# Up projection with x stationary, and u turned to channels on partitions by a transposing DMA

## The chip, the cores and the metric

The kernel runs on one core of one Trainium2 chip. The metric is the device time of one execution in microseconds (us), taken as the median of several runs. A profile is one execution recorded by the hardware profiler; its span goes from the first to the last instruction.

## The reference

One encoder layer on 256 tokens of width 2048, in fp32. The part that the change touches is the convolutional gated feed-forward at its end:

```
def conv_gated_ffn(h, w_up, conv_w, conv_b, w_down):     # h = rms_norm(x): (1, 256, 2048)
    u = h @ w_up                                         # w_up: (2048, 11264)
    up_ = jnp.pad(u, ((0, 0), (1, 1), (0, 0)))
    u = up_[:, :-2] * conv_w[0] + up_[:, 1:-1] * conv_w[1] + up_[:, 2:] * conv_w[2] + conv_b
    gate, val = jnp.split(u, 2, axis=-1)
    return (jax.nn.silu(gate) * val) @ w_down            # w_down: (5632, 2048)
```

Ahead of it stand RMS norm, an input projection, window attention over 8 heads, a bidirectional gated linear attention and the output projection `wo`.

## The kernel before

TensorE works with pairs of numbers. Every fp32 operand is split into a rounded part `hi` (type fp32r) and a rest `lo`; a product of two fp32 matrices is three matmuls, hi by hi, hi by lo and lo by hi, summed in PSUM. Weights come from HBM in units of 128 partitions x 1024 columns (512 KB). For each unit `weights()` issues the load on SyncE's queue (tile `r`, four buffers), ScalarE writes `h` (four buffers) and VectorE writes `l` (three buffers). These two instructions are put forward in the schedule by `high_priority`; otherwise the order of each engine's instructions is set at build time by a scheduler from the order of the program, and each engine runs its list in that order.

The stages follow one another on TensorE: ten chunks of the input projection with attention and linear attention between them, `wo`, the up projection, the down projection. In the input projection, `wo` and the down projection a 128x128 block of the activations is stationary and 512 weight columns move. In the up projection it is the other way: 128x128 weight blocks are stationary, so that u comes out with channels on partitions and tokens along the row, as the convolution over tokens wants it. The loop goes over the 44 channel blocks `f` and the two halves (gate and value), 88 blocks of 128 channels, each with 16 blocks of the contraction. For each of these there are two matmuls: the weight's hi part against x's hi and lo side by side (512 columns, L630), and the weight's lo part against x's hi (256 columns, L631). Both write one PSUM tile `pu` of a pool of four.

A block is then finished by one ScalarE copy (L633) and VectorE instructions: the two halves of `pu` are added, the token's norm factor `rbc` is multiplied on (it was spread over the partitions by a small matmul, `pb`), three instructions make the convolution, and then follow SiLU, the product of gate and value, and the split into `g`, which the down projection keeps stationary.

The names in the rows: `hu`, `lu`, `ru` are the parts and the raw tile of a unit of w_up, `hd`, `ld`, `rd` those of w_down; `xs` holds the split x; `ptx` are TensorE transposes of the last columns of `wo`'s result; `u`, `c` are the block before and after the convolution.

Of the kernel before, what the change touches and what calls it, by code (L numbers as in the profile page):

```python
# [8 lines left out]
F32 = mybir.dt.float32  # L9
F32R = mybir.dt.float32r  # L10
BF16 = mybir.dt.bfloat16
U32 = mybir.dt.uint32
AF = mybir.ActivationFunctionType
ALU = mybir.AluOpType
AX = mybir.AxisListType
# [3 lines left out]
P = 128  # L19
T = 256  # L20
DM = 2048
NKT = DM // P
# [4 lines left out]
NFF = DFF // P  # L27
# [32 lines left out]
def tile_hymba_layer(  # L60
# [15 lines left out]
    nc = tc.nc  # L76
    V, S, G, PE = nc.vector, nc.scalar, nc.gpsimd, nc.tensor
# [9 lines left out]
    def arena(shape, dt, name):  # L87
        return ar.tile(shape, dt, name=name, tag="ar")

    def work(shape, dt, name, tag="wk", bufs=2):  # L90
        return wk.tile(shape, dt, name=name, tag=tag, bufs=bufs)

    def acc(name):
        return pacc.tile([P, 512], F32, name=name, tag="acc")

    def aux(name):
        return paux.tile([P, 512], F32, name=name, tag="aux")
# [14 lines left out]
    def split(hi, lo, src):  # L112
        S.activation(hi, src, AF.Copy)
        V.tensor_tensor(lo, src, hi.bitcast(F32), ALU.subtract)
# [56 lines left out]
    def token_square(c):  # L171

        r = raw(f"xq{c}")
        nc.sync.dma_start(out=r, in_=xr[c])
        for t in range(2):
            junk = work([P, 512], BF16, "junkx", "jk", 1)
            S.activation(junk, r[:, t * 512 : t * 512 + 512], AF.Square, accum_out=ssq1[:, t, c : c + 1])

    def token_norm():
# [290 lines left out]
    def retrieve(h):  # L470
        po = aux(f"pog{h}")
        for t in range(2):
            for s in range(2):
                product(
                    po[:, t * T : t * T + T], both(atr, A, h, 2 * s + t), both(vgr, A, s, slice(h * T, h * T + T)),
                    start=(s == 0), stop=(s == 1),
                )
        o = o_sb[:, h]
        S.activation(o.rearrange("p t e -> p (t e)"), po, AF.Copy)
        ss = sm.tile([P, 2], F32, name="sso", tag="sso", bufs=4)  # L480
        rs = sm.tile([P, 2], F32, name="rso", tag="rso", bufs=4)
        for t in range(2):
            junk = work([P, T], BF16, "junko", "jk", 1)
            S.activation(junk, o[:, t], AF.Square, accum_out=ss[:, t : t + 1])
        inv_sqrt(rs, ss, 1.0 / T, EPS, 2)
        yield
        for t in range(2):
            V.scalar_tensor_tensor(
                out=o[:, t], in0=o[:, t], scalar=rs[:, t : t + 1], in1=sg[:, t, h * T : h * T + T], op0=ALU.mult, op1=ALU.mult
            )  # L490
        yield
        pt = aux(f"pto{h}")
        for t in range(2):
            for e in range(2):
                PE.transpose(pt[:, e * T + t * P : e * T + t * P + P], o[:, t, e * P : e * P + P], ident)
        split(ogh[:, 2 * h : 2 * h + 2], ogl[:, 2 * h : 2 * h + 2], pt.rearrange("p (k s) -> p k s", k=2))
# [68 lines left out]
    first = 0  # L565
    for c in range(4):
        xres = raw(f"xres{c}")
        nc.sync.dma_start(out=xres[:, :1024], in_=xr[c])
        ps = [acc(f"po{c}{t}") for t in range(2)]
        for u in range(NKT // 2):  # L570
            if c == 0:
                run_hooks(10, u)
            hi, lo = weights(wo, first, 1024, f"o{c}{u}")
            first += P * 1024
            for k in range(2):
                kt = 2 * u + k
                sh, sl = (oah, oal) if kt < 8 else (ogh, ogl)
                for t in range(2):
                    a = sh[:, kt % 8, t * P : t * P + P]
                    b = sl[:, kt % 8, t * P : t * P + P]  # L580
                    wh, wl = hi[:, k * 512 : k * 512 + 512], lo[:, k * 512 : k * 512 + 512]
                    PE.matmul(ps[t], a, wh, start=(kt == 0), stop=False)  # L582
                    PE.matmul(ps[t], a, wl, start=False, stop=False)  # L583
                    PE.matmul(ps[t], b, wh, start=False, stop=(kt == NKT - 1))  # L584
        x1c = x1[c // 2][:, c % 2]
        for t in range(2):
            V.tensor_tensor(x1c[:, t], ps[t], xres[:, t * 512 : t * 512 + 512], ALU.add)
            junk = work([P, 512], BF16, "junk2", "jk", 1)
            S.activation(junk, x1c[:, t], AF.Square, accum_out=ssq2[:, t, c : c + 1])
        for i in range(2):  # L590
            pt = aux(f"ptx{c}{i}")
            for j in range(2):
                for t in range(2):
                    n = (2 * i + j) * P
                    PE.transpose(pt[:, j * T + t * P : j * T + t * P + P], x1c[:, t, n : n + P], ident)
            for j in range(2):
                n = 4 * c + 2 * i + j
                h = xs[n // 4][:, n % 4, 0]
                S.activation(h, pt[:, j * T : j * T + T], AF.Copy, scale=g2[:, n : n + 1])
                V.scalar_tensor_tensor(  # L600
                    out=xs[n // 4][:, n % 4, 1], in0=pt[:, j * T : j * T + T], scalar=g2[:, n : n + 1],
                    in1=h.bitcast(F32), op0=ALU.mult, op1=ALU.subtract,
                )
# [1 line left out]
    rstd2 = pers.tile([P, 2], F32, name="rstd2")  # L605
    V.tensor_reduce(s2, ssq2, AX.X, ALU.add)
    inv_sqrt(rstd2, s2, 1.0 / DM, EPS, 2)
    pb = aux("pb")
    for t in range(2):
        dg = work([P, P], F32, f"dg{t}")  # L610
        V.tensor_scalar(dg, ident, rstd2[:, t : t + 1], None, op0=ALU.mult)
        PE.matmul(pb[:, t * P : t * P + P], ones, dg, start=True, stop=True)
    rbc = pers.tile([P, T], F32, name="rbc")
    V.tensor_copy(rbc, pb[:, :T])


    gts = [arena([P, 2, 4, T], F32R, f"g{i}") for i in range(NFF // 4)]
    first = 0
    for f in range(NFF):
        cs = []  # L620
        for half in range(2):
            n = f + half * NFF
            pu = acc(f"pu{n}")
            for u in range(2):
                hi, lo = weights(wu, first, 1024, f"u{n}{u}")
                first += P * 1024
                for k in range(8):
                    wh, wl = hi[:, k * P : k * P + P], lo[:, k * P : k * P + P]
                    x2 = xs[2 * u + k // 4][:, k % 4].rearrange("p a s -> p (a s)")
                    PE.matmul(pu, wh, x2, start=(u == 0 and k == 0), stop=False)  # L630
                    PE.matmul(pu[:, T:], wl, x2[:, :T], start=False, stop=(u == 1 and k == 7))  # L631
            ut = work([P, T], F32, f"u{n}", "pT")
            S.activation(ut, pu[:, T:], AF.Copy)  # L633
            V.tensor_tensor(ut, ut, pu[:, :T], ALU.add)  # L634
            V.tensor_tensor(ut, ut, rbc, ALU.mult)  # L635
            c = work([P, T], F32, f"c{n}", "sc", 3)
            V.tensor_scalar(c, ut, cw[:, 1, n : n + 1], cb[:, n : n + 1], op0=ALU.mult, op1=ALU.add)  # L637
            V.scalar_tensor_tensor(  # L638
                out=c[:, 1:T], in0=ut[:, 0 : T - 1], scalar=cw[:, 0, n : n + 1], in1=c[:, 1:T], op0=ALU.mult, op1=ALU.add
            )  # L640
            V.scalar_tensor_tensor(  # L641
                out=c[:, 0 : T - 1], in0=ut[:, 1:T], scalar=cw[:, 2, n : n + 1], in1=c[:, 0 : T - 1], op0=ALU.mult, op1=ALU.add
            )
            cs.append(c)
        S.activation(cs[0], cs[0], AF.Silu)
        V.tensor_tensor(cs[1], cs[0], cs[1], ALU.mult)
        gt = gts[f // 4]
        S.activation(gt[:, 0, f % 4], cs[1], AF.Copy)
        V.tensor_tensor(gt[:, 1, f % 4], cs[1], gt[:, 0, f % 4].bitcast(F32), ALU.subtract)


    first = 0
    for c in range(4):
        ps = [acc(f"pd{c}{t}") for t in range(2)]
        for u in range(NFF // 2):
            hi, lo = weights(wd, first, 1024, f"d{c}{u}")
            first += P * 1024
            for k in range(2):
                kt = 2 * u + k
                gt = gts[kt // 4]  # L660
                for t in range(2):
                    a = gt[:, 0, kt % 4, t * P : t * P + P]
                    b = gt[:, 1, kt % 4, t * P : t * P + P]
                    wh, wl = hi[:, k * 512 : k * 512 + 512], lo[:, k * 512 : k * 512 + 512]
                    PE.matmul(ps[t], a, wh, start=(kt == 0), stop=False)  # L665
                    PE.matmul(ps[t], a, wl, start=False, stop=False)  # L666
                    PE.matmul(ps[t], b, wh, start=False, stop=(kt == NFF - 1))  # L667
# [111 lines left out]
```

## Time and profile before

| | |
|---|---|
| median of 3 runs | 1086.81 us (1085.79 to 1088.91) |
| profiled execution, its own time | 1088.95 us |
| its span | 1087.2 us, 14981 instructions |
| TensorE busy | 1077.7 us (99%) |
| VectorE busy | 769.5 us (71%) |
| ScalarE busy | 535.0 us (49%) |
| DMA | 205.06 MB, 189 GB/s in the mean |
| granted TensorE clock | 0.998 |

Busy time of TensorE counts a matmul until its result has drained, so that neighbours overlap; what a stage costs is read from the starts of its matmuls.

### The profile page before, as it was taken

How to read it: one execution, taken by the hardware profiler on the slowest of the kernel's cores; microseconds unless marked ns; L12 is line 12 of the kernel's file. 1: busy time of each engine (PE TensorE's matmuls, PEld its weight loads, DVE VectorE, ACT ScalarE, POOL GpSimd, SP SyncE). 2: the span in 40 equal slices, each digit the busy share in tenths (PEclk: the TensorE clock that was granted, in tenths of full speed). 3: DMA queues.
4: the chain of work that ended last, by engine and by line, in shares of the span. 5: the costliest groups of instructions: out<-in, count | busy, mean ns of one | idle time of the engine just before them, and what ended most of it. 6: DMA issues, size and time to landing. Idle time of an engine off the chain costs nothing.

```text
span 1087.2 us, 14981 instructions
## 1 busy us (share of the span) xinstructions
PE 1077.7 (99%) x5608; PEld 918.2 (84%) x5608; DVE 769.5 (71%) x1174; ACT 535.0 (49%) x796; POOL 11.3 (1%) x16
## 2 busy tenths in 40 slices
PE   9999999999999999999999999999999999999998
PEld 7789888888888888888888888888888888888886
DVE  6688776755555888888888888888888544444443
ACT  6646575764445544444444444444444433333331
POOL 0010000010000000000000000000000000000000
PEclk9999999999999999999999999999999999999999
DMA  9765545445656656665565565655666666666662
GB/s 343 266 195 163 172 125 161 131 137 191 195 194 224 189 187 189 183 191 182 186 192 182 188 187 183 192 179 189 186 184 192 193 194 211 194 214 194 211 194 80
DMA packets 58616, 205.06 MB, mean 189 GB/s; under 512 B 6640, under 2 KB 7664, under 8 KB 58416
## 3 DMA queue, kind: packets, MB, share of 16 engines
q1 hardware_dynamic: 58256, 203.97, 59.3%
q8 instruction: 44, 0.72, 0.3%
q14 instruction: 28, 0.23, 0.1%
q10 hardware_dynamic: 288, 0.14, 0.0%
HBM read 201.99 MB, written 2.10 MB: 188 GB/s over the span
## 4 chain that ended last, share of the span: by engine, by line
PE 96%; DMA 2%; DVE 1%; ACT 0%; issue 0%; DVEq 0%; SPq 0%; ACTq 0%
PE pu L630 30%; PE pu L631 15%; PE pd L667 7%; PE pd L665 7%; PE pd L666 7%; PE po L583 3%; PE po L584 3%; PE po L582 3%; PE pvg L226 1%; PE pvg L227 1%; PE pgt L228 1%; PE pgt L226 1%; PE pvg L228 1%; PE pgt L227 1%; PE pqa L227 1%; PE pqa L228 1%
## 5 line engine op out<-in xcount | busy, mean ns | idle before, releaser
L630 PE MATMUL pu<-xs,hu 128*128 128x512 f32 x1408 | 497.4, 399 | 0.0
L631 PE MATMUL pu<-xs,lu 128*128 128x256 f32 x1408 | 395.2, 281 | 0.0
L630 PEld LDWEIGHTS pu<-xs,hu 128*128 128x128 f32 x1408 | 264.4, 188 | 65.6
L108 ACT ACTIVATE hu<-ru 128x1024 fp32r<-128x1024 f32 x176 | 186.9, 1062 | 253.4 <-PE pu L630 143.6
L631 PEld LDWEIGHTS pu<-xs,lu 128*128 128x128 f32 x1408 | 266.0, 189 | 0.2
L109 DVE TENSOR_TENSOR lu<-ru,hu 128x1024 fp32r<-128x1024 f32 x176 | 215.2, 1223 | 47.5 <-PE pu L631 41.1
L109 DVE TENSOR_TENSOR ld<-rd,hd 128x1024 fp32r<-128x1024 f32 x88 | 107.8, 1225 | 117.5 <-PE pd L666 114.0
L108 ACT ACTIVATE hd<-rd 128x1024 fp32r<-128x1024 f32 x88 | 93.6, 1064 | 143.8 <-PE pd L667 135.0
L666 PE MATMUL pd<-ld,g 128*128 128x512 f32 x352 | 136.9, 389 | 0.0
L665 PE MATMUL pd<-hd,g 128*128 128x512 f32 x352 | 136.9, 389 | 0.0
L667 PE MATMUL pd<-hd,g 128*128 128x512 f32 x352 | 136.9, 389 | 0.0
L667 PEld LDWEIGHTS pd<-hd,g 128*128 128x128 f32 x352 | 66.1, 188 | 13.8
L666 PEld LDWEIGHTS pd<-ld,g 128*128 128x128 f32 x352 | 66.1, 188 | 13.8
L665 PEld LDWEIGHTS pd<-hd,g 128*128 128x128 f32 x352 | 66.1, 188 | 13.5
L109 DVE TENSOR_TENSOR lo<-ro,ho 128x1024 fp32r<-128x1024 f32 x32 | 38.8, 1223 | 38.4 <-ACT ho L108 27.8
L108 ACT ACTIVATE ho<-ro 128x1024 fp32r<-128x1024 f32 x32 | 33.8, 1060 | 46.4 <-DMA ro<-in_wo_dram 33.0
L634 DVE TENSOR_TENSOR u<-u,pu 128x256 f32<-128x256 f32 x88 | 36.9, 420 | 13.8 <-ACT u L633 13.3
L641 DVE SCALAR_TENSOR_TENSOR c<-u,prm_sb,c 128x255 f32<-128x255 f32 x88 | 42.5, 484 | 3.0
L638 DVE SCALAR_TENSOR_TENSOR c<-u,prm_sb,c 128x255 f32<-128x255 f32 x88 | 41.9, 477 | 0.1
L637 DVE TENSOR_SCALAR c<-u,prm_sb 128x256 f32<-128x256 f32 x88 | 36.2, 412 | 3.0
L635 DVE TENSOR_TENSOR u<-u,rbc 128x256 f32<-128x256 f32 x88 | 37.1, 421 | 1.5
L633 ACT ACTIVATE u<-pu 128x256 f32<-128x256 f32 x88 | 32.1, 365 | 0.0
(221 smaller groups left out, 1390.5 us busy)
## 6 DMA issues: line engine op xcount, KB each, us to landing
ru<-in_wu_dram SPq DMA_DIRECT2D x176, 512.0 KB, 4.0
rd<-in_wd_dram SPq DMA_DIRECT2D x88, 512.0 KB, 4.3
ro<-in_wo_dram SPq DMA_DIRECT2D x32, 512.0 KB, 3.6
riqa<-in_wi_dram SPq DMA_DIRECT2D x16, 512.0 KB, 3.6
rivg<-in_wi_dram SPq DMA_DIRECT2D x16, 512.0 KB, 3.9
rigt<-in_wi_dram SPq DMA_DIRECT2D x16, 512.0 KB, 3.5
riqg<-in_wi_dram SPq DMA_DIRECT2D x8, 512.0 KB, 3.5
rilk<-in_wi_dram SPq DMA_DIRECT2D x10, 408.0 KB, 3.5
```

The lines of the kernel that those rows point to most:

```text
L108: S.activation(hi[:, :cols], r[:, :cols], AF.Copy)
L109: V.tensor_tensor(lo[:, :cols], r[:, :cols], hi[:, :cols].bitcast(F32), ALU.subtract)
L630: PE.matmul(pu, wh, x2, start=(u == 0 and k == 0), stop=False)
L631: PE.matmul(pu[:, T:], wl, x2[:, :T], start=False, stop=(u == 1 and k == 7))
L634: V.tensor_tensor(ut, ut, pu[:, :T], ALU.add)
L635: V.tensor_tensor(ut, ut, rbc, ALU.mult)
L637: V.tensor_scalar(c, ut, cw[:, 1, n : n + 1], cb[:, n : n + 1], op0=ALU.mult, op1=ALU.add)
L638: V.scalar_tensor_tensor(out=c[:, 1:T], in0=ut[:, 0 : T - 1], scalar=cw[:, 0, n : n + 1], in1=c[:, 1:T], op0=ALU.mult, op1=ALU.add)
L641: V.scalar_tensor_tensor(out=c[:, 0 : T - 1], in0=ut[:, 1:T], scalar=cw[:, 2, n : n + 1], in1=c[:, 0 : T - 1], op0=ALU.mult, op1=ALU.add)
L665: PE.matmul(ps[t], a, wh, start=(kt == 0), stop=False)
L666: PE.matmul(ps[t], a, wl, start=False, stop=False)
L667: PE.matmul(ps[t], b, wh, start=False, stop=(kt == NFF - 1))
```

## The change

The up projection is turned round. It goes over 22 chunks `ch` of 512 columns (256 gate channels and the 256 value channels that belong to them; the host orders w_up so). For each chunk a 128-token block of x is stationary and 512 weight columns move, three matmuls for each contraction block and token block, into two PSUM tiles, one for each 128 tokens. The result has tokens on partitions, so the norm factor is a per-partition scale of the evacuation (`us`, ScalarE). To get channels on partitions, VectorE copies the 16-bit halves of each fp32 of `us` into two planes (`pl`, 128 x 1024 of 16 bits), a transposing DMA on ScalarE's queue turns each `pl` (`uT`), and ScalarE writes the two planes back interleaved, which is fp32 again (`v`). The middle tap of the convolution and the bias go to ScalarE, for two blocks of channels there is one SiLU, one product and one split. `turn` of a chunk stands behind unit 1 and `convolve` behind unit 3 of the next chunk; those of the last chunk stand in the first column of the down projection. The matmul `pb` is gone. The pool of scratch tiles has four buffers of tag "wk" in place of two, and the scrap tiles of the squares (`junk`) use it too.

```
-    def work(shape, dt, name, tag="wk", bufs=2):
-        return wk.tile(shape, dt, name=name, tag=tag, bufs=bufs)
+    def work(shape, dt, name, tag="wk", bufs=None):
+        return wk.tile(shape, dt, name=name, tag=tag, bufs=bufs or (4 if tag == "wk" else 2))
...
-            junk = work([P, 512], BF16, "junk2", "jk", 1)
+            junk = work([P, 512], BF16, "junk2")
...
+    def up(ch):
+        ps = [acc(f"pu{ch}{t}") for t in range(2)]
+        for u in range(NKT // 2):
+            hi, lo = weights(wu, ch * DM * 512 + u * P * 1024, 1024, f"u{ch}_{u}")
+            for k in range(2):
+                kt = 2 * u + k
+                wh, wl = hi[:, k * 512 : k * 512 + 512], lo[:, k * 512 : k * 512 + 512]
+                for t in range(2):
+                    a = xs[kt // 4][:, kt % 4, 0, t * P : t * P + P]
+                    b = xs[kt // 4][:, kt % 4, 1, t * P : t * P + P]
+                    PE.matmul(ps[t], a, wh, start=(kt == 0), stop=False)
+                    PE.matmul(ps[t], a, wl, start=False, stop=False)
+                    PE.matmul(ps[t], b, wh, start=False, stop=(kt == NKT - 1))
+            if ch and u == 1:
+                turn(ch - 1)
+            if ch and u == 3:
+                convolve(ch - 1)
...
+            us = work([P, 512], F32, f"us{ch}{t}", "wk", 4)
+            pl = work([P, 2, 512], U16, f"pl{ch}{t}", "wk", 4)
+            with tc.high_priority(offset=1500):
+                S.activation(us, ps[t], AF.Copy, scale=rstd2[:, t : t + 1])
+            V.tensor_copy(pl, us.bitcast(U16).rearrange("p (n h) -> p h n", h=2))
...
+    def turn(ch):
+        ut = work([P, 2, 4, T], U16, f"uT{ch}", "pT")
+        flat = ut.rearrange("p h j s -> p (h j) s")
+        for t in range(2):
+            nc.scalar.dma_start_transpose(flat[:, :, t * P : t * P + P], planes[ch][t].rearrange("p h n -> p (h n)"))
...
+            v = work([P, 2, T], F32, f"v{ch}{half}", "sc", 3)
+            S.activation(
+                v.rearrange("p j s -> p (j s)").bitcast(U16).rearrange("p (n h) -> p h n", h=2),
+                turned[ch][:, :, 2 * half : 2 * half + 2].rearrange("p h j s -> p h (j s)"), AF.Copy,
             )
...
+                S.activation(c[:, j], v[:, j], AF.Identity, bias=cb[:, n : n + 1], scale=cw[:, 1, n : n + 1])
```

On TensorE, in the middle of the up projection, a contraction block of one block of 128 channels took a 512-column and a 256-column matmul:

```order
L630 MATMUL pu_4570<-xs_2461,hu_4573 128x512
L631 MATMUL pu_4570<-xs_2461,lu_4574 128x256
L630 MATMUL pu_4570<-xs_2461,hu_4573 128x512
L631 MATMUL pu_4570<-xs_2461,lu_4574 128x256
L630 MATMUL pu_4570<-xs_2461,hu_4573 128x512
L631 MATMUL pu_4570<-xs_2461,lu_4574 128x256
```

Now a contraction block of four blocks of channels takes six matmuls of 512 columns, three for each token tile; 12 of them belong to one unit of weights:

```order
L626 MATMUL pu_4595<-hu_4_4696,xs_2462 128x512
L627 MATMUL pu_4595<-lu_4_4697,xs_2462 128x512
L628 MATMUL pu_4595<-hu_4_4696,xs_2462 128x512
L626 MATMUL pu_4596<-hu_4_4696,xs_2462 128x512
L627 MATMUL pu_4596<-lu_4_4697,xs_2462 128x512
```

In all there were 2816 matmuls of the up projection, and now there are 2112, all of 512 columns.

On ScalarE, in the middle of the up projection, the list before held two conversions of weights (`hu`) for each block, and between them the copies of `pu` and the work on `c` and `g`:

```order
L633 ACTIVATE u_4725<-pu_4680 128x256
L108 ACTIVATE hu_4850<-ru_4848 128x1024
L108 ACTIVATE hu_4872<-ru_4870 128x1024
L633 ACTIVATE u_4782<-pu_4737 128x256
L648 ACTIVATE g_3189<-c_4729 128x256
```

Now the two evacuations of a chunk, its two transposing DMAs and the joining of its planes stand in one list with the conversions for the next chunk (`hu_3` is unit 3 of that chunk):

```order
L109 ACTIVATE hu_2_3743<-ru_2_3741 128x1024
L638 ACTIVATE us_3692<-pu_3521,rstd_3172 128x512
L109 ACTIVATE hu_3_3761<-ru_3_3759 128x1024
L638 ACTIVATE us_3696<-pu_3522,rstd_3172 128x512
L646 DMA_TRANSPOSE uT_3738<-pl_3693 128x8x128
L109 ACTIVATE hu_4_3801<-ru_4_3799 128x1024
L646 DMA_TRANSPOSE uT_3738<-pl_3697 128x8x128
L109 ACTIVATE hu_5_3819<-ru_5_3817 128x1024
L653 ACTIVATE v_3777<-uT_3738 128x2x512
L660 ACTIVATE c_3779<-v_3777,prm_sb 128x256 x2
L653 ACTIVATE v_3786<-uT_3738 128x2x512
L109 ACTIVATE hu_6_3837<-ru_6_3835 128x1024
```

The conversion of unit 6 moved behind the joining, and the first joining instruction waits for both transposing DMAs.

On VectorE the same stretch of the change has the copies into planes behind `lu_2`, and the convolution between `lu_5` and `lu_6`:

```order
L110 TENSOR_TENSOR lu_2_3744<-ru_2_3741,hu_2_3743 128x1024
L639 COPY pl_3693<-us_3692 128x1024
L639 COPY pl_3697<-us_3696 128x1024
L110 TENSOR_TENSOR lu_3_3762<-ru_3_3759,hu_3_3761 128x1024
L110 TENSOR_TENSOR lu_4_3802<-ru_4_3799,hu_4_3801 128x1024
L110 TENSOR_TENSOR lu_5_3820<-ru_5_3817,hu_5_3819 128x1024
L661 SCALAR_TENSOR_TENSOR c_3779<-v_3777,prm_sb,c_3779 128x255 x2
L664 SCALAR_TENSOR_TENSOR c_3779<-v_3777,prm_sb,c_3779 128x255 x2
L110 TENSOR_TENSOR lu_6_3838<-ru_6_3835,hu_6_3837 128x1024
```

So `lu_6` stands behind instructions that read what the transposing DMAs bring.

## Rows read from the trace of the kernel before

**Rows 1.** The page: busy time of each engine in its span.

```profile
span 1087.2 us, 14981 instructions
PE 1077.7 (99%) x5608; PEld 918.2 (84%) x5608; DVE 769.5 (71%) x1174; ACT 535.0 (49%) x796; POOL 11.3 (1%) x16
```

**Rows 2.** The page: the chain that ended last, by engine.

```profile
PE 96%; DMA 2%; DVE 1%; ACT 0%; issue 0%; DVEq 0%; SPq 0%; ACTq 0%
```

**Rows 3.** TensorE's waits, longest and shortest of six: total us, times, longest us.

```profile
PE pqa L226 <- ACT hiqa L108: 1.5, 1, 1.5
...
PE pkv L227 <- DVE likv L109: 0.5, 1, 0.5
```

**Rows 4.** Windows: stretch, its length, busy us (instructions) of PE, PEld, DVE, ACT, POOL, clock, DMA share, GB/s.

```profile
0.00:40.00 40.00, 35.31 (x146) 27.61 (x147) 21.61 (x35) 27.42 (x50) 0.90 (x5) 0.98 0.88 319
400.00:600.00 200.00, 200.00 (x1133) 173.33 (x1133) 172.22 (x283) 95.49 (x141) 0.00 (x0) 1.00 0.60 187
600.00:622.55 22.55, 22.55 (x129) 19.54 (x129) 19.43 (x33) 10.80 (x16) 0.00 (x0) 1.00 0.59 187
```

**Rows 5.** Timeline of TensorE around the up and down projections: start us, us, instruction.

```profile
345.00 0.39 PE L630 MATMUL pu<-xs,hu 128*128 128x512 f32 x1
...
350.37 0.82 PE L595 MATMUL ptx<-prm_sb,x 128*128 128x128 f32 x6
350.94 0.36 PE L631 MATMUL pu<-xs,lu 128*128 128x256 f32 x1
...
353.46 0.61 PE L612 MATMUL pb<-dg,ones 128*128 128x128 f32 x4
353.83 0.36 PE L631 MATMUL pu<-xs,lu 128*128 128x256 f32 x1
...
843.61 0.40 PE L665 MATMUL pd<-hd,g 128*128 128x512 f32 x1
...
1082.77 0.39 PE L667 MATMUL pd<-hd,g 128*128 128x512 f32 x1
```

**Rows 6.** Timeline of TensorE in the attention: 256-column matmuls one behind another.

```profile
119.82 0.28 PE L120 MATMUL pss<-kvr,qT 128*128 128x256 f32 x1
...
120.18 0.28 PE L120 MATMUL pss<-kvr,qT 128*128 128x256 f32 x1
```

**Rows 7.** Groups, 600 to 622.55 us: busy us, mean ns of one | idle before.

```profile
L108 ACT ACTIVATE hu<-ru 128x1024 fp32r<-128x1024 f32 x8 | 8.5, 1062 | 11.8 <-PE pu L630 7.1 <-issue 4.8
L633 ACT ACTIVATE u<-pu 128x256 f32<-128x256 f32 x4 | 1.5, 364 | 0.0
...
L109 DVE TENSOR_TENSOR lu<-ru,hu 128x1024 fp32r<-128x1024 f32 x8 | 9.8, 1224 | 2.0 <-PE pu L631 2.0
...
L638 DVE SCALAR_TENSOR_TENSOR c<-u,prm_sb,c 128x255 f32<-128x255 f32 x4 | 1.9, 477 | 0.0
```

**Rows 8.** Groups of the whole span with the shapes that the change uses.

```profile
L114 DVE TENSOR_TENSOR pT<-pp,pT 128x512 fp32r<-128x512 f32 x8 | 5.5, 684 | 1.7 <-ACT pT L113 1.7
L113 ACT ACTIVATE pT<-pp 128x512 fp32r<-128x512 f32 x8 | 4.7, 586 | 4.9 <-PE pp L335 4.9
L234 ACT ACTIVATE qa_sb<-pqa,rstd 128x512 f32<-128x512 f32 x4 | 2.7, 686 | 2.6 <-PE pqa L228 2.6
L386 ACT ACTIVATE na<-na 128x512 f32<-128x512 f32 x4 | 2.4, 620 | 2.5 <-DVE na L385 2.5
L390 DVE TENSOR_TENSOR mn<-mn,na 128x1024 f32<-128x1024 f32 x2 | 2.4, 1222 | 1.6 <-ACT na L387 1.6
L392 ACT ACTIVATE gh<-mn 128x1024 fp32r<-128x1024 f32 x2 | 2.1, 1046 | 0.0
```

**Rows 9.** DMA queues (packets, MB, share) and issues (KB each, median us to landing).

```profile
q1 hardware_dynamic: 58256, 203.97, 59.3%
...
ru<-in_wu_dram SPq DMA_DIRECT2D x176, 512.0 KB, 4.0
...
out_dram<-x SPq DMA_DIRECT2D x7, 256.0 KB, 3.6
```

More of the change, by code (lines that the diff above doesn't have):

```diff
@@ L12 @@
 U32 = mybir.dt.uint32
+U16 = mybir.dt.uint16
 AF = mybir.ActivationFunctionType
@@ L175, in token_square @@
         for t in range(2):
-            junk = work([P, 512], BF16, "junkx", "jk", 1)
+            junk = work([P, 512], BF16, "junkx")
             S.activation(junk, r[:, t * 512 : t * 512 + 512], AF.Square, accum_out=ssq1[:, t, c : c + 1])
@@ L482, in retrieve @@
         for t in range(2):
-            junk = work([P, T], BF16, "junko", "jk", 1)
+            junk = work([P, T], BF16, "junko")
             S.activation(junk, o[:, t], AF.Square, accum_out=ss[:, t : t + 1])
@@ L607, in tile_hymba_layer @@
     inv_sqrt(rstd2, s2, 1.0 / DM, EPS, 2)
[L608 to L614, printed above, removed]
-    gts = [arena([P, 2, 4, T], F32R, f"g{i}") for i in range(NFF // 4)]
-    first = 0
-    for f in range(NFF):
+    gts = [arena([P, 2, 4, T], F32R, f"g{i}") for i in range(NFF // 4)]
@@ new lines, in tile_hymba_layer @@
+    planes, turned = {}, {}
+    def up(ch):
[15 more added lines that the diff above has]
+                convolve(ch - 1)
+        planes[ch] = []
+        for t in range(2):
[4 more added lines that the diff above has]
+            V.tensor_copy(pl, us.bitcast(U16).rearrange("p (n h) -> p h n", h=2))
+            planes[ch].append(pl)
@@ L620, in tile_hymba_layer, with convolve @@
+    def turn(ch):
+        ut = work([P, 2, 4, T], U16, f"uT{ch}", "pT")
+        flat = ut.rearrange("p h j s -> p (h j) s")
+        for t in range(2):
+            nc.scalar.dma_start_transpose(flat[:, :, t * P : t * P + P], planes[ch][t].rearrange("p h n -> p (h n)"))
+        turned[ch] = ut
+    def convolve(ch):
         cs = []
         for half in range(2):
[L622 to L639, printed above, removed]
-            )
@@ L641, in tile_hymba_layer @@
-            V.scalar_tensor_tensor(
-                out=c[:, 0 : T - 1], in0=ut[:, 1:T], scalar=cw[:, 2, n : n + 1], in1=c[:, 0 : T - 1], op0=ALU.mult, op1=ALU.add
-            )
+            v = work([P, 2, T], F32, f"v{ch}{half}", "sc", 3)
+            S.activation(
+                v.rearrange("p j s -> p (j s)").bitcast(U16).rearrange("p (n h) -> p h n", h=2),
+                turned[ch][:, :, 2 * half : 2 * half + 2].rearrange("p h j s -> p h (j s)"), AF.Copy,
+            )
+            c = work([P, 2, T], F32, f"c{ch}{half}", "sc", 3)
@@ new lines, in convolve @@
+            for j in range(2):
+                n = half * NFF + 2 * ch + j
+                S.activation(c[:, j], v[:, j], AF.Identity, bias=cb[:, n : n + 1], scale=cw[:, 1, n : n + 1])
+                V.scalar_tensor_tensor(
+                    out=c[:, j, 1:T], in0=v[:, j, 0 : T - 1], scalar=cw[:, 0, n : n + 1], in1=c[:, j, 1:T], op0=ALU.mult, op1=ALU.add
+                )
+                V.scalar_tensor_tensor(
+                    out=c[:, j, 0 : T - 1], in0=v[:, j, 1:T], scalar=cw[:, 2, n : n + 1], in1=c[:, j, 0 : T - 1], op0=ALU.mult, op1=ALU.add
+                )
@@ L646, in tile_hymba_layer @@
         V.tensor_tensor(cs[1], cs[0], cs[1], ALU.mult)
+        f = 2 * ch
         gt = gts[f // 4]
-        S.activation(gt[:, 0, f % 4], cs[1], AF.Copy)
-        V.tensor_tensor(gt[:, 1, f % 4], cs[1], gt[:, 0, f % 4].bitcast(F32), ALU.subtract)
+        split(gt[:, 0, f % 4 : f % 4 + 2], gt[:, 1, f % 4 : f % 4 + 2], cs[1])
+    for ch in range(NFF // 2):
+        up(ch)
     first = 0
@@ L655, in tile_hymba_layer @@
         for u in range(NFF // 2):
+            if c == 0 and u == 1:
+                turn(NFF // 2 - 1)
+            if c == 0 and u == 3:
+                convolve(NFF // 2 - 1)
             hi, lo = weights(wd, first, 1024, f"d{c}{u}")
@@ L742 @@
     w = a["w_up"][0]
-    wu = w.reshape(2, 8, P, 2, NFF, P).transpose(4, 3, 0, 2, 1, 5).reshape(-1)
+    w = w.reshape(DM, 2, NFF // 2, 2 * P).transpose(2, 0, 1, 3).reshape(NFF // 2, DM, 512)
+    wu = np.concatenate([_units(w[c], [2] * (NKT // 2)) for c in range(NFF // 2)])
     w = a["w_down"][0]
```

## The prediction

> **What bounds the kernel now.** The page comes first: TensorE is busy for 1077.7 of 1087.2 us [rows 1], and the chain that ended last runs through TensorE for 96% [rows 2]. Busy time of overlapping matmuls proves little, so the waits come next: TensorE waited for others six times only, 1.5 us at the longest and 0.5 at the shortest, and no instruction of the up projection is among them [rows 3]. The windows show who else is near: in the up projection VectorE is busy for 172 of 200 us, ScalarE for 95, DMA at a share of 0.60 [rows 4]. So this stage goes at the pace at which TensorE issues matmuls at full clock, and a change is worth what it takes from that pace, unless it makes another engine late.
>
> The pace is read from starts. The up projection begins at 345.00, the down projection at 843.61 [rows 5]: 498.61 us. In it lie transposes (six pushed the next matmul back by 0.57 us, so eight by about 0.76) and `pb` (0.37). The other 497.5 us hold 1408 pairs of a 512-column and a 256-column matmul, 353.3 ns a pair. The down projection has 1056 matmuls of 512 columns from 843.61 to 1082.77 [rows 5]: 239.16 / 1055 = 226.7 ns each. Where 256-column matmuls follow each other, three starts take 0.36 us, 120 ns each [rows 6]. At 2.4 GHz the columns alone are 213.3 and 106.7 ns, so each matmul costs 13 ns beyond its columns. A pair would then be 346.7 ns; the up projection pays 6.6 ns more, for which no row names a cause.
>
> **TensorE's part.** The columns stay the same: 1408 x 768 = 2112 x 512. The count falls from 2816 to 2112, 704 fewer, at 13.3 ns 9.4 us. `pb` saves 0.37. What becomes of the unnamed 6.6 ns a pair (9.3 us in all) isn't known. If it goes, the stage takes 2112 x 0.2267 + 0.76 = 479.5 us, 19.1 less. If it stays with the columns, it is 9.3 more: 488.8, 9.8 less. The down projection, whose form the new loop has, doesn't pay it, but VectorE is much quieter there. I take the middle, 484.2 us and a saving of 14.4.
>
> Here a rule of the Trainium skill speaks against the change. The row says that a matmul costs 13 ns over its columns at either width [rows 5, 6]. The page "TensorE: Matmul & The Clock Gate" (Part 1, "Wait — 56ns, not 53.3ns?") gives a fixed cost of about 2.5 ns per warm matmul. By that 704 fewer matmuls would save 1.8 us, by the rows 9.4. The trace doesn't agree with the page for these fp32 operands; the sum goes by the rows.
>
> **VectorE and ScalarE.** A chunk of the change does the work of four blocks, which now last 22.55 us with VectorE busy for 19.43 and ScalarE for 10.80 [rows 4]. New on VectorE: eight `lu` of 1.224, two plane copies priced at the 1222 ns of a 128x1024 instruction, eight convolution taps of 0.477, a product and a split of 0.684 [rows 7, 8]: 9.8 + 2.4 + 3.8 + 1.4 = 17.4 us of a chunk of 22. That is lighter than now. New on ScalarE: eight `hu` of 1.062, two evacuations of 0.686, two joins at 1.046, four middle taps at 0.364, SiLU at 0.620, a split at 0.586 [rows 7, 8]: 8.5 + 1.4 + 2.1 + 1.5 + 0.6 + 0.6 = 14.7 us, and two DMA issues. Neither is full; what these cost is nothing as long as the lists keep their order in time. The traffic grows by 2 x 256 KB a chunk, 24 GB/s on about 190; the first 40 us moved 319 GB/s [rows 4].
>
> **The wait that the change adds.** The join waits for two transposing DMAs, and behind it in ScalarE's list stand `hu_6`, `hu_7`; behind the taps in VectorE's list stands `lu_6`. TensorE waits for those. With 12 matmuls a unit (2.75 us), let a chunk end at 0. `us` of the first token block runs to 0.8, `hu_3`, whose buffer comes free at 0, to 1.9, the second `us` to 2.6; VectorE does `lu_2` to 1.3, plane copies to 2.5 and 3.8. So the first DMA is issued at 2.6 and, with `hu_4` between them, the second at 3.8. On the other side: TensorE begins unit 6 at 16.5, so `hu_6` has to be done by about 15.5 for `lu_6` to follow. Ahead of it are join, two taps, join (2.8 us) and itself (1.06): the DMAs must have landed by 11.6 us.
>
> No row shows a transposing DMA. From below: 256 KB at the 319 GB/s of the first stretch are 0.8 us. From above: 58256 packets took 59.3% of 16 engines' 1087.2 us [rows 1, 9], 0.177 us each. Cut into 256-byte pieces (128 elements of 16 bits), a transfer is 1024 of these, 11.3 us on 16 engines. The nearest row by size and source is the store of the output, 256 KB from 128 rows of 2 KB in SBUF, 3.6 us to landing [rows 9]. I take it: the second lands at 7.4, with 4.2 us to spare. If ScalarE were held for each whole transfer, it would be 2.6 + 3.6 + 1.06 + 3.6 = 10.9, still in time. At 11.3 us each, one after the other, it is 25.2, 13.6 late in each chunk.
>
> The Trainium skill has two rules on this that disagree. "DMA: Bandwidth & Descriptors" (Latency and other measured facts) gives 261 GB/s for a transposing DMA; an estimate from it is 1.0 us, all hidden. "VectorE: DVE Perf Modes" (The three transpose paths) gives 1309 ns for a 128x128 block; an estimate for eight in a row is 10.5 us, 21 for the two, landing at 23.6. No row here tells them apart.
>
> The early stages: `junk` in the shared pool and the moved order cost or give at most small waits, since TensorE has only 9.5 us without work in all [rows 1]. I put 0 there, plus or minus 2.
>
> **Sum.** The profiled execution took 1088.95 us, 1.75 beyond its span. 1088.95 - 14.4 = 1074.6. It lies 2.1 us above the median of the runs shown, so in terms of that median 1086.8 - 14.4 = 1072.4.
>
> **The rivals.**
> - The transposes land late. For it speaks that nothing in this trace measures them and that ScalarE's list is strict; against it the 3.6 us of the nearest row. Late by one us costs 22 us in all, so the gain is gone at 0.65 us late, a landing at 12.3 us, that is about 4.8 us for each in a row. At the upper bound 22 x 13.6 = 299 us: 1371. The page's block figure, if blocks follow each other, would give 22 x 12.0 = 264 us: 1336. In between it is anything from 1073 up.
> - The matmul count is worth next to nothing, because what TensorE pays goes with columns. Then only 1.8 us is saved, 1085, no change that can be told. The 120 ns and 226.7 ns rows speak against it. This is the time that the page's 2.5 ns would give.
> - The unnamed 6.6 ns goes entirely: 1067.7. The down projection speaks for it.
>
> **How the numbers follow.** A measurement of this kernel can tell about 0.3% from no change, 3.3 us. Transposes hidden and the saving between 9.8 and 19.1: 0.59, with its own range 1066 to 1078. Late by a little, so that the time lies between 1078 and 1130: 0.15, a third of it within 0.3% of before. Late by much: 0.18. The count worth nothing: 0.04. Something in the early stages: 0.04. Faster 0.62, same 0.09, slower 0.29. The range reaches from 1065 into the little-late cases, to 1130, and leaves out the heavy ones.
>
> **What would show it.** Right: starts of up-projection matmuls 227 to 232 ns apart without gaps, the first `hu_6` of a chunk waiting for a buffer and not for a DMA, the span from the first up to the first down matmul 479 to 489 us. Wrong: waits of TensorE for `hu` or `lu` of units 6 and 7 in every chunk, ended in turn by a join that waited for a DMA; or ScalarE standing at a transposing DMA for several us.

## The result, and the profile after

The changed kernel takes 1199.79 us in the median of 4 runs (1195.81 to 1202.54), the kernel before 1086.3 us: a ratio of 1.104 (95% interval 1.100 to 1.108). The forecast was 1072.4 us in a range of 1065 to 1130. It was the rival "the transposes land late" that came true, further out than the range reached: the prediction had put late landings beyond 1130 us at 0.18.

The page of the changed kernel, with the lines that answer to [rows 1], [rows 2] and [rows 9], and the group of the join (busy us, mean ns | idle before):

```profile
span 1200.7 us, 13525 instructions
...
q10 hardware_dynamic: 46752, 11.68, 7.7%
...
PE 59%; DMA 22%; ACT 8%; DVE 6%; issue 3%; ACTq 1%; SPq 0%; DVEq 0%
...
L653 ACT ACTIVATE v<-uT 128x1024 uint16<-128x1024 uint16 x44 | 59.2, 1346 | 153.1 <-DMA uT<-pl 153.1
...
uT<-pl ACTq DMA_TRANSPOSE x44, 7.4
```

The chain that ended last ran through TensorE for 96%; now it is 59%, and 22% of the span stands at a DMA, nearly all of it at the turned planes. ScalarE waited 153.1 us for them at the join, and TensorE then waited 68.7 us for `hu`. TensorE's waits in the changed kernel (total us, times, longest us), beside [rows 3]:

```profile
PE pu L626 <- ACT hu L109: 68.7, 19, 7.3
PE pu L627 <- DVE lu L110: 13.0, 21, 0.8
PE pd L695 <- ACT hd L109: 4.5, 1, 4.5
```

About one wait a chunk, 19 long ones and 21 short ones. One chunk on ScalarE shows how it comes about (timeline of ScalarE and its queue: start us, us, instruction, idle before):

```profile
615.69 1.25 ACTq L646 DMA_TRANSPOSE uT<-pl  x1
617.07 1.06 ACT L109 ACTIVATE hu<-ru 128x1024 fp32r<-128x1024 f32 x1 [1.43 <-PE pu L628]
617.09 3.15 ACTq L646 DMA_TRANSPOSE uT<-pl  x1
620.36 1.06 ACT L109 ACTIVATE hu<-ru 128x1024 fp32r<-128x1024 f32 x1 [2.23 <-DVE lu L110]
630.08 1.34 ACT L653 ACTIVATE v<-uT 128x1024 uint16<-128x1024 uint16 x1 [8.66 <-DMA uT<-pl]
...
633.65 1.98 ACT L109 ACTIVATE hu<-ru 128x1024 fp32r<-128x1024 f32 x2
```

On TensorE the next chunk begins at 613.1, the end of this one. The DMAs were issued 2.6 and 4.0 us later, as forecast (2.6 and 3.8). ScalarE was free for the join at 621.4, 4.3 us after the second issue, but the join could begin only at 630.08, 17.0 us after the end of the chunk and 13.0 after the second issue. `hu_6` and `hu_7`, the last row, stand behind it. On TensorE (the same columns):

```profile
613.12 0.39 PE L626 MATMUL pu<-hu,xs 128*128 128x512 f32 x1
...
629.67 0.39 PE L628 MATMUL pu<-hu,xs 128*128 128x512 f32 x1
634.74 0.79 PE L626 MATMUL pu<-hu,xs 128*128 128x512 f32 x1 [4.68 <-ACT hu L109]
636.00 0.79 PE L627 MATMUL pu<-lu,xs 128*128 128x512 f32 x1 [0.47 <-DVE lu L110]
636.59 0.63 PE L628 MATMUL pu<-hu,xs 128*128 128x512 f32 x1
637.01 0.63 PE L626 MATMUL pu<-hu,xs 128*128 128x512 f32 x1
...
641.85 0.40 PE L627 MATMUL pu<-lu,xs 128*128 128x512 f32 x1
642.08 0.39 PE L628 MATMUL pu<-hu,xs 128*128 128x512 f32 x1
```

TensorE ran out of weights at unit 6, 16.8 us after the chunk's end. After the pause its matmuls start 0.42 to 0.43 us apart instead of 0.23. The window from 636 to 640 says why (the columns of [rows 4]):

```profile
636.00:640.00 4.00, 4.00 (x9) 3.13 (x10) 3.73 (x7) 3.14 (x6) 0.00 (x0) 0.50 0.52 146
```

The granted clock is 0.50 from 636 to 640, that is 1.2 GHz, after a stretch from 630 to 634.7 in which TensorE did nothing, and full again from about 641.5. So a late landing can be paid twice: once as the pause, once as half clock.

This chunk is one of the late ones. All 44 landings, counted from the issue of each:

```profile
DMA to landing us min/median/max: 4.7/7.4/14.5
```

The two DMAs of a chunk differ: taken apart, the first lands 6.0 us after its issue in the median of 22, the second 11.4 us (6.8 to 14.5). It is the second that the join waits for.

### The profile page after: what moved, and what is told of

Same layout as the page of the kernel before. It is cut to its first block, busy times and chain, and to the rows that moved or that the text cites. A ratio compares the mean times of both kernels' runs of the same rounds, so it can differ in the third digit from the quotient of the medians.

```text
span 1200.7 us, 13525 instructions
## 1 busy us (share of the span) xinstructions
PE 1106.9 (92%) x4900; PEld 906.3 (75%) x4900; DVE 682.2 (57%) x907; ACT 626.3 (52%) x840; POOL 14.6 (1%) x16
## 3 DMA queue, kind: packets, MB, share of 16 engines
q10 hardware_dynamic: 46752, 11.68, 7.7%
## 4 chain that ended last, share of the span: by engine, by line
PE 59%; DMA 22%; ACT 8%; DVE 6%; issue 3%; ACTq 1%; SPq 0%; DVEq 0%
DMA uT<-pl 21%; PE pd L696 6%; PE pd L697 6%; PE pd L695 6%; PE pu L627 5%; PE pu L626 5%; ACT v L653 5%; PE pu L628 5%; DVE lu L110 4%; PE po L584 2%; PE po L585 2%; PE po L583 2%; ACT hu L109 2%; DVE pl L639 1%; PE pvg L229 1%
## 5 line engine op out<-in xcount | busy, mean ns | idle before, releaser
L626 PE MATMUL pu<-hu,xs 128*128 128x512 f32 x704 | 284.3, 414 | 68.7 <-ACT hu L109 68.7
L627 PE MATMUL pu<-lu,xs 128*128 128x512 f32 x704 | 289.3, 411 | 13.0 <-DVE lu L110 13.0
L628 PE MATMUL pu<-hu,xs 128*128 128x512 f32 x704 | 286.0, 406 | 0.0
L110 DVE TENSOR_TENSOR lu<-ru,hu 128x1024 fp32r<-128x1024 f32 x176 | 214.6, 1222 | 108.7 <-PE pu L627 50.1
L109 ACT ACTIVATE hu<-ru 128x1024 fp32r<-128x1024 f32 x176 | 180.9, 1050 | 99.1 <-PE pu L628 41.6
L626 PEld LDWEIGHTS pu<-hu,xs 128*128 128x128 f32 x704 | 141.5, 201 | 107.3 <-ACT hu L109 77.0
L627 PEld LDWEIGHTS pu<-lu,xs 128*128 128x128 f32 x704 | 139.4, 198 | 50.8 <-DVE lu L110 21.5
L628 PEld LDWEIGHTS pu<-hu,xs 128*128 128x128 f32 x704 | 139.8, 199 | 29.3
L653 ACT ACTIVATE v<-uT 128x1024 uint16<-128x1024 uint16 x44 | 59.2, 1346 | 153.1 <-DMA uT<-pl 153.1
L661 DVE SCALAR_TENSOR_TENSOR c<-v,prm_sb,c 128x255 f32<-128x255 f32 x88 | 42.6, 484 | 168.7 <-ACT c L660 168.3
L660 ACT ACTIVATE c<-v,prm_sb 128x256 f32<-128x256 f32 x88 | 47.7, 589 | 0.7
L638 ACT ACTIVATE us<-pu,rstd 128x512 f32<-128x512 f32 x44 | 29.8, 678 | 21.6 <-PE pu L628 21.6
```

The costliest lines, as they stand in the source:

```text
L109: S.activation(hi[:, :cols], r[:, :cols], AF.Copy)
L110: V.tensor_tensor(lo[:, :cols], r[:, :cols], hi[:, :cols].bitcast(F32), ALU.subtract)
L638: S.activation(us, ps[t], AF.Copy, scale=rstd2[:, t : t + 1])
L653: S.activation(v.rearrange("p j s -> p (j s)").bitcast(U16).rearrange("p (n h) -> p h n", h=2), turned[ch][:, :, 2 * half : 2 * half + 2]. ...
L660: S.activation(c[:, j], v[:, j], AF.Identity, bias=cb[:, n : n + 1], scale=cw[:, 1, n : n + 1])
L661: V.scalar_tensor_tensor(out=c[:, j, 1:T], in0=v[:, j, 0 : T - 1], scalar=cw[:, 0, n : n + 1], in1=c[:, j, 1:T], op0=ALU.mult, op1=ALU.add)
```

## The experiments

The theory after this reading was **late join**: TensorE's own pace is as forecast, and everything lost is ScalarE standing at the join for the landing, with the conversions for TensorE behind it in its list. The rivals: **too much work** on ScalarE or VectorE, and **traffic**, transposing DMAs that starve the weight loads or hold ScalarE at their issue. Ratios are to the kernel before, which took 1085.5 to 1085.7 us in the median beside these runs.

**e1_no_transpose.**

```
-            nc.scalar.dma_start_transpose(flat[:, :, t * P : t * P + P], planes[ch][t].rearrange("p h n -> p (h n)"))
...
-                turned[ch][:, :, 2 * half : 2 * half + 2].rearrange("p h j s -> p h (j s)"), AF.Copy,
+                planes[ch][half], AF.Copy,
```

> The two transposing DMAs of a chunk are left out, and the join reads the planes of its own token block instead of the turned ones, so u is not turned and the output is not the reference's. All else stays: 2112 matmuls, evacuations, plane copies, joins, taps. Theory 'late join' (TensorE's own pace is as forecast, and all that is lost is ScalarE standing at the join for the landing, with the conversions of units 6 and 7 behind it): the stage falls from about 614 us to about 480, the whole to 1063 to 1068 us. Rival 'too much work' (evacuations, joins and taps fill ScalarE or VectorE, so that conversions come late anyway): stays above 1090.

Measured: 1067.28 us, ratio 0.983 (0.982 to 0.985). TensorE has no wait in the up projection. "Too much work" is out: all of the new evacuations, plane copies, joins and taps fit. (The stage of the changed kernel, from the first up to the first down matmul, is 342.07 to 946.76, 604.7 us, not the 614 of the expectation.)

**e2_unread.** Only the second of these two edits: the DMAs run, and nobody reads what they bring.

> The transposing DMAs run as before, but the join reads the planes and not what they bring, so nobody waits for them (output not the reference's). Theory 'late join': within 5 us of the run without them, 1063 to 1072 us, since only the wait cost time. Rival 'traffic' (the transposing DMAs hold up the weight loads, or hold ScalarE while they are issued, long enough that TensorE starves without any wait at the join): above 1100 us, with waits for loads or a ScalarE that stands at the issue.

Measured: 1067.37 us, ratio 0.983 (0.981 to 0.985). TensorE has four groups of waits in this kernel, all ahead of the up projection; the longest and the shortest:

```profile
PE warm L163 <- DVE mhalf L158: 1.1, 1, 1.1
...
PE pkv L227 <- ACT hikv L109: 0.3, 1, 0.3
```

The landings are nearly as slow as in the changed kernel (issues and landings of the turned planes from 400 to 900 us; the second of a pair lands after 10.3 us in the median of 22):

```profile
L646 ACTq DMA_TRANSPOSE uT<-pl x40: 1247/1651/3747, 410.1 to 825.0; - x40
...
DMA to landing us min/median/max: 4.5/7.5/12.2
```

So "traffic" is out too: the same DMAs cost 0.1 us, which is within the noise, when nobody waits for them, even though ScalarE's queue is held up to 3.7 us at an issue.

**e3_join_later.** Writing `convolve` further down in the program doesn't move the join: behind unit 6 instead of unit 3, it is still put between the conversions of units 5 and 6 in ScalarE's list. So the join got a dependency on the conversion of unit 1 of the chunk after the next (the last two chunks' joins, not shown, follow conversions of the down projection):

```
-            if ch and u == 3:
-                convolve(ch - 1)
+            if ch > 1 and u == 1:
+                convolve(ch - 2, hi)
...
+        one = sm.tile([P, 1], F32, name=f"one{ch}", tag="one", bufs=2)
+        V.tensor_scalar(one, after[:, 0:1].bitcast(F32), 0.0, 1.0, op0=ALU.mult, op1=ALU.add)
...
-                turned[ch][:, :, 2 * half : 2 * half + 2].rearrange("p h j s -> p h (j s)"), AF.Copy,
+                turned[ch][:, :, 2 * half : 2 * half + 2].rearrange("p h j s -> p h (j s)"), AF.Copy, scale=one,
```

> The whole computation. The join of a chunk takes a scale of 1.0 that is computed from a column of the converted unit 1 of the chunk after the next, so that it can't stand ahead of that conversion in ScalarE's list; a chunk's DMAs then have about 17 us instead of 8 before the join asks for them. Theory 'late join': 1064 to 1076 us, faster than the kernel before by 1 to 2%, with no TensorE wait of more than 1 us in the up projection. Rival 'traffic': above 1100, since the DMAs still take 13 us a pair and the same bandwidth.

Measured: 1067.08 us, ratio to the kernel before 0.983 (0.981 to 0.984). This is the whole computation, and it is faster than both kernels. TensorE waits only ahead of `wo`, three groups in all:

```profile
PE pkv L227 <- ACT hikv L109: 1.3, 2, 1.0
...
PE pkv L228 <- DVE likv L110: 0.5, 1, 0.5
```

ScalarE issues a chunk's DMAs at 606.43 and 608.77 and asks for them 13.2 us after the second; the join waits for `one`, not for a DMA:

```profile
606.43 1.25 ACTq L646 DMA_TRANSPOSE uT<-pl  x1
...
608.77 1.83 ACTq L646 DMA_TRANSPOSE uT<-pl  x1
...
621.96 1.46 ACT L655 ACTIVATE v<-uT,one 128x1024 uint16<-128x1024 uint16 x1 [0.22 <-DVE one L652]
```

"Late join" stands, but on e2: there the landings are as slow as before, and only the waiting is gone. In e3 they are shorter too, 5.2 us in the median against 7.4, and the second of a pair takes 5.6 instead of 11.4. An estimate from that (issue 4.6 us after the chunk's end, plus 5.6) is 10.2 us, in time for the old place of the join as well, so e3 alone doesn't tell a later join from earlier landings.

What goes with the shorter landings is the distance between the two issues: 2.3 us here, 1.4 in the changed kernel. The first chunk of each kernel is the other way round. In e3 its two issues are 1.5 us apart, in the changed kernel 2.4 (DMAs of the first chunk, e3 first):

```profile
L646 ACTq DMA_TRANSPOSE uT<-pl x2: 1322/2244/3167, 366.7 to 368.2; - x2
...
DMA to landing us min/median/max: 6.7/9.1/11.4
```

```profile
L646 ACTq DMA_TRANSPOSE uT<-pl x2: 1932/2094/2255, 366.7 to 369.1; - x2
...
DMA to landing us min/median/max: 5.6/6.2/6.8
```

So the slow second landing follows the close issue in both kernels. No run moves the second issue alone, so that this would have been enough is not shown.

**e4_tail.** Behind the end of the changed kernel, when no weights are loaded any more:

```
+    nc.scalar.dma_start_transpose(ta, row)
+    nc.scalar.dma_start_transpose(ta[:, :4], row[:, :512])
+    nc.scalar.dma_start_transpose(ta[:, :1], row[:, :128])
+    nc.scalar.dma_start(out=ta.rearrange("p a b -> p (a b)"), in_=row)
...
+    for i in range(4):
+        nc.sync.dma_start(out=rs[i], in_=wd[i * P * 1024 : (i + 1) * P * 1024].rearrange("(p c) -> p c", p=P))
+    nc.scalar.dma_start_transpose(ta, row)
+    nc.scalar.dma_start_transpose(tb, row)
```

> The changed kernel with a string of transposing DMAs behind its end, each waiting for the one before unless said: two at once, one alone, half of one (4 blocks of 128x128), one block, a plain copy of the same 256 KB inside SBUF, one alone, and two at once beside four 512 KB loads. Theory 'pieces' (a transposing DMA is cut into 256-byte pieces and the pair goes one after the other whatever else runs): alone 5 to 7 us, half 3 to 4, one block about 2, the pair 10 to 13, with or without loads; plain copy about 3. Rival 'contention' (it is slow only beside the weight loads): alone 2 to 4 us, the pair 4 to 6, and 12 or more only beside the loads.

The chain gives each from issue to landing (start us, us): a whole one beside a second, a whole one alone, a half, one block, the plain copy, and a whole one alone again.

```profile
1209.64 2.80 DMA ta<-src
1212.46 2.75 DMA ta<-src
1215.23 2.32 DMA ta<-src
1217.57 2.30 DMA ta<-src
1219.95 2.28 DMA ta<-src
1222.25 2.74 DMA ta<-src
```

Alone, a transposing DMA of 256 KB is as quick as a plain copy of the same bytes to within 0.5 us, and two at once don't disturb each other: 2.80 us for the first, 2.8 for the second. Beside four loads the two took 7.2 and 9.2 us, the longest landing of `ta` and of `tb`:

```profile
DMA to landing us min/median/max: 2.3/2.7/7.2
...
DMA to landing us min/median/max: 2.8/6.0/9.2
```

Each of these is a single reading. "Pieces" in the form stated (slow by itself) is wrong. "Contention" is right in that it is slow only beside the loads, though the pair stays under the 12 us that it asked for. A plain copy was not run beside the loads, so what in a transposing DMA suffers from them is left open.

**e5_load_pieces.** The same place, a transposing DMA issued with four loads, in pieces of 4 KB and of 1 KB:

```
+            nc.sync.dma_start(
+                out=rs[i].rearrange("p (k c) -> p k c", k=pieces),
+                in_=wd[i * 1024 * P : (i + 1) * 1024 * P].rearrange("(k p c) -> p k c", p=P, k=pieces),
+            )
+        nc.scalar.dma_start_transpose(ta[:, :blocks], row[:, : blocks * P])
```

> The changed kernel with four measurements behind its end, one after the other: a transposing DMA of 8 blocks and one of 2 blocks (256 and 64 KB), each issued together with four 512 KB loads in pieces of 4 KB, and then the same two beside loads in pieces of 1 KB. Alone they took 2.75 us (8 blocks) and 2.3 us (1 block). Theory 'turns' (on each DMA engine the two queues take turns piece by piece, so that each 256-byte piece waits for one piece of a load): 8 blocks beside 4 KB 8 to 10 us, 2 blocks beside 4 KB 4.5 to 6, 8 blocks beside 1 KB 5 to 6.5, 2 blocks beside 1 KB about 3. Rival 'bytes' (the transposing DMA lands when the loads ahead of it are through, whatever the pieces): 7 to 9 us in all four.

VectorE's idle time before it could read the result, which begins within 0.3 us of the issue (8 blocks and 2 blocks beside 4 KB, 8 and 2 beside 1 KB):

```profile
1202.40 0.35 DVE L725 CAST ta<-rt 128x1 uint16<-128x1 f32 x2 [10.00 <-DMA ta<-src]
...
1212.18 0.35 DVE L725 CAST ta<-rt 128x1 uint16<-128x1 f32 x2 [6.88 <-DMA ta<-src]
...
1222.21 0.35 DVE L725 CAST ta<-rt 128x1 uint16<-128x1 f32 x2 [7.34 <-DMA ta<-src]
...
1230.87 0.35 DVE L725 CAST ta<-rt 128x1 uint16<-128x1 f32 x2 [5.84 <-DMA ta<-src]
```

Neither theory hits all four. A DMA engine has 64 pieces of 8 blocks and 16 of 2. The 48 more cost 3.1 us beside 4 KB pieces, 65 ns each, 1.5 us beside 1 KB pieces, 31 ns, and alone about 9 ns each (2.80 against 2.30 us for 56 pieces). So a piece costs more the larger the loads' pieces are, as "turns" says, but less than the 0.177 us of a mean packet in the prediction; without these costs 5.8 us are left beside 4 KB and 5.3 beside 1 KB, against 2.3 for one block alone, which "turns" doesn't explain. These four are single readings too.

**e6_loads_2k.** The changed kernel with w_up in pieces of 2 KB:

```
+            nc.sync.dma_start(out=r.rearrange("p (k c) -> p k c", k=2), in_=src.rearrange("(k p c) -> p k c", k=2, p=P))
```

> The changed kernel with the loads of w_up in pieces of 2 KB instead of 4 KB (the weights lie in HBM block by block, so a row of a unit is two pieces); the list order is not touched. Theory 'turns': a transposing DMA beside them lands in about 5 us instead of 7.4, the pair about 8 after the first is issued instead of 13, by about 11 us after the end of a chunk, where 11.6 was the latest by the prediction: 1066 to 1100 us. Rival 'bytes': no change, 1190 to 1205.

Measured: 1171.07 us, ratio to the kernel before 1.0785 (1.0765 to 1.0805): 29 us below the changed kernel. The second DMA of a pair lands after 10.1 us in the median of 22 where it took 11.4, and TensorE's wait for `hu` falls from 68.7 to 48.1 us:

```profile
PE pu L630 <- ACT hu L113: 48.1, 19, 5.4
PE pu L631 <- DVE lu L114: 15.0, 21, 0.8
```

Smaller pieces help in the direction of "turns" and by less than it said. The second landing is 1.3 us earlier, and the kernel takes 1.3 us a chunk less, as it should if the join's wait is what costs.

**e7_before_grouped.** The kernel before, to settle the 6.6 ns a pair that the prediction had no cause for:

```
                 for k in range(8):
...
                     PE.matmul(pu, wh, x2, start=(u == 0 and k == 0), stop=False)
-                    PE.matmul(pu[:, T:], wl, x2[:, :T], start=False, stop=(u == 1 and k == 7))
+                for k in range(8):
...
+                    PE.matmul(pu[:, T:], wl, x2[:, :T], start=False, stop=(u == 1 and k == 7))
```

> The kernel before; within a unit of w_up the eight 512-column matmuls come first and then the eight 256-column ones, instead of taking turns. The open 6.6 ns a pair: theory 'alternation' (it comes from a 256-column matmul between 512-column ones, too short to cover the next load of a stationary block): the pair falls from 353.3 to about 347 ns, 1077 us. Rival 'other engines' (VectorE's and ScalarE's traffic in this stage) or 'columns': no change, 1085 to 1087.

Measured: 1080.26 us, ratio 0.995 (0.993 to 0.996). The first matmuls of the up and of the down projection:

```profile
341.86 1.98 PE L630 MATMUL pu<-xs,hu 128*128 128x512 f32 x8
...
834.83 0.40 PE L668 MATMUL pd<-hd,g 128*128 128x512 f32 x1
```

The stage takes 492.97 us instead of 498.61; less the same 1.13 us for transposes and `pb` that is 349.3 ns a pair instead of 353.3. Taking turns between the widths costs 4.0 of the 6.6 ns; 2.6 stay open, and the kernel stays 3 us above the 1077 that "alternation" stood for.

**e8_tensor_transposes.** x stationary, u turned by TensorE:

```
-            V.tensor_copy(pl, us.bitcast(U16).rearrange("p (n h) -> p h n", h=2))
...
+                    PE.transpose(pv[:, j * T + t * P : j * T + t * P + P], planes[ch][t][:, n : n + P], ident)
```

> x stationary as in the changed kernel, but u is turned by TensorE: eight 128x128 transposes of fp32 a chunk into two PSUM tiles, from which ScalarE takes the middle tap and VectorE the others. No planes, no transposing DMAs, no join. 176 transposes; six of them pushed the next matmul back by 0.57 us in the kernel before, so 17 us in all. If only the wait at the join was wrong with the change: 1067 + 17 = 1084 us, about the kernel before, with no waits of TensorE. Rival (x stationary itself is slow in this stage): above 1095.

Measured: 1086.44 us, ratio 1.001 (1.000 to 1.002), no wait of TensorE in the stage. The stage (start of the first up matmul, start of the first down matmul):

```profile
343.96 0.39 PE L626 MATMUL pu<-hu,xs 128*128 128x512 f32 x1
...
842.37 0.39 PE L692 MATMUL pd<-hd,g 128*128 128x512 f32 x1
```

498.4 us. In e3 it goes from 342.11 to 821.75, 479.6:

```profile
342.11 0.39 PE L626 MATMUL pu<-hu,xs 128*128 128x512 f32 x1
...
821.75 0.39 PE L697 MATMUL pd<-hd,g 128*128 128x512 f32 x1
```

So 176 transposes cost 18.8 us, 107 ns each, and eat the whole gain of the turned loop.

## Why the prediction was wrong

**TensorE's part was right.** The sum had 479.5 to 488.8 us for the stage, by whether the unnamed 6.6 ns stay. In e3 it is 479.6 us against 498.6 [rows 5]: they go, and the saving is 19.0, not the 14.4 of the middle. e7 shows the larger part of it, 4.0 ns: the turned loop has no 256-column matmuls between its 512-column ones. With the join out of the way the kernel takes 1067.1 us, and the rival that named this case said 1067.7. By the Trainium skill's 2.5 ns per matmul ("TensorE: Matmul & The Clock Gate", Part 1, "Wait — 56ns, not 53.3ns?") an estimate of 1.8 us would have been saved; the runs don't agree with it for these fp32 operands, which take 226.7 ns for 512 columns in e3 too (479.64 us less 0.76 for the transposes, over 2112 matmuls).

**VectorE and ScalarE were right in sum, not in parts.** A plane copy took 690 ns where 1222 was priced, a join 1346 where 1046, a middle tap 589 where 364. In e1 a chunk of 21.76 us has VectorE busy for 15.4 us and ScalarE for 15.1 (283.6 and 277.6 of 400 us), where the sums had 17.4 and 14.7; it all fits.

**The wait was seen, and its clock was right.** The prediction put the issues at 2.6 and 3.8 us after the end of a chunk (2.6 and 4.0 measured), the latest harmless landing at 11.6, and the end of TensorE's supply at 16.5 (16.8 measured). Its sign of being wrong, TensorE waiting for the last units of each chunk behind a join that waits for a DMA, is what the trace shows. (Of the kernel before it says that TensorE waited six times; the view has six groups and seven waits, and nothing hangs on it.)

**The step that failed is the duration of the transposing DMA.** It was between 0.8 and 11.3 us, and "the nearest row by size and source is the store of the output ... 3.6 us to landing. I take it", with the second landing at 7.4 us after the chunk's end. In the chunk shown the second landed at 17.0. Over all 22 chunks the first of a pair takes 6.0 us and the second 11.4 in the median, so that the second lands at about 15.4.

The row was not at fault for want of traffic: six of the seven stores were issued while w_down was being loaded, at as high a DMA share as in the up projection (kernel before, the columns of [rows 4]; then the landings of these six):

```profile
890.00:1030.00 140.00, 140.00 (x620) 115.91 (x619) 67.22 (x58) 55.33 (x52) 0.00 (x0) 1.00 0.65 205
```

```profile
DMA to landing us min/median/max: 3.4/4.3/5.3
```

So a store of the same bytes lands in 3.4 to 5.3 us beside loads, where the transposing DMA, 2.75 us alone (e4), takes 6.0 and 11.4. They differ in kind: the store goes in rows of 2 KB on SyncE's queue. The 46752 packets on ScalarE's queue, less the 288 of before, are 1056 for each of 44 DMAs of 256 KB, nearly all of 256 bytes. The upper bound counted in just these pieces, 1024 at the mean packet's time, and its 11.3 us is what the second of a pair takes; that it fits is partly luck, since e5 has 31 to 65 ns for a piece and not 177. The pair, besides, was added up as if the second took no longer than the first.

Both pages of the Trainium skill miss it from two sides. The estimate from "VectorE: DVE Perf Modes" (The three transpose paths), taken block by block, was 10.5 us for what takes 2.75 alone. The estimate from "DMA: Bandwidth & Descriptors" (Latency and other measured facts) was 1.0 us, while alone one block of the eight already takes 2.30 us (e4).

**The price of being late held for the wait and had nothing for the clock.** The prediction had 22 us for each us late. At 15.4 us the second landing is 3.8 late, an estimate of 84 us; TensorE's waits for `hu`, `lu` and `hd` are 86.2. But the changed kernel loses 1199.8 - 1067.1 = 132.7 against e3. For the other 46.5 us, 2.1 a chunk, the prediction had no term. Most of it is the time at 1.2 GHz after pauses: the trace has 17 such stretches in the up projection and at the start of the down projection, 95.6 us in all. TensorE stood still for 15.8 us of that, so that half of the remaining 79.8, an estimate of 39.9 us, is lost. That leaves 6.6 us without a cause.

**What stays open:** why a landing beside loads takes 5.8 to 6.9 us even for two blocks (e5), why the second of a pair needs 11.4 us in the changed kernel and 5.6 in e3, and the last 2.6 ns a pair. What e2 and e3 show is that the wait for the landing costs the time; why the landing is slow beside the loads is only in part explained. The larger pool of scratch tiles was not tried alone.

## What to carry to other kernels

When a new DMA stands on an engine's list ahead of work that another engine needs, price its landing from a row of its own kind in the traffic of its own stage. Here a store of the same bytes beside the same kind of loads was no model for it. Ask for the distance between the issue and the first reader before asking for the gain: asked for 13.2 us after the second issue the DMAs were free (e3, where they also landed sooner), asked for 4.3 us after it they cost 133 us. The scheduler put the reader close behind the DMA wherever the program had it; a dependency on later work kept them apart. TensorE's pauses, 86 us in all, cost about 40 more at 1.2 GHz after them.

## What the runs showed of the hardware

- A transposing DMA of 128 x 1024 16-bit values inside SBUF takes 2.75 us alone, one block of 128 x 128 takes 2.30, a plain copy 2.28 (e4). Beside 512 KB loads the large one takes 4.7 to 14.5 us (changed kernel): in the median 6.0 for the first of a pair and 11.4 for the second issued 1.4 us later, against 5.1 and 5.6 where the issues are 2.3 us apart (e3). Smaller pieces of the loads shorten it, 10.0 to 7.3 us from 4 KB to 1 KB pieces (e5).
- Its issue holds ScalarE's queue for 1.25 us, and up to 3.7 us for the second of a pair (e2).
- At 2.4 GHz a 512-column matmul of these operands starts every 226.7 ns; a 512-column and a 256-column one in turn take 4.0 ns more than in rows of their own kind (353.3 against 349.3 ns a pair, e7).
- VectorE copies 1024 16-bit values a partition out of every second place in 690 ns; ScalarE writes 1024 of them into every second place in 1346 ns, against 1050 ns for 1024 fp32 values (changed kernel).
